# A hybrid decoder layer: all projections ahead of the attention by seven block products, convolution tiles inside it

## The chip, the cores and the metric

The kernel runs on one core of a Trainium2 chip. The time is that of one execution on the device, in microseconds (us). The core's engines work side by side, each through its own queue of instructions: TensorE (PE; its weight loads are listed as PEld), VectorE (DVE), ScalarE (ACT), GpSimd (POOL) and SyncE (SP), which here only starts transfers (DMA).

## What is computed

One layer of a hybrid decoder: a norm, one combined projection into a gated short convolution and an attention, an output projection, and a gated feed-forward part. There are 2048 positions, a model width of 1024, 8 heads of 64, a convolution width of 512 and a feed-forward width of 2816. The reference, cut to this:

```python
h = rms_norm(x, g_mix)
z = h @ w_in
u, gb, gc, q, k, v = jnp.split(z, splits, axis=-1)     # 512 columns each

y_conv = gb * short_conv(gc * u, conv_w)               # causal, width 3

q = rms_norm(q.reshape(B, S, N_HEADS, HEAD_DIM), g_q) * (HEAD_DIM ** -0.5)
k = rms_norm(k.reshape(B, S, N_HEADS, HEAD_DIM), g_k)
y_attn = dilated_mixture(q, k, v)       # branches (128,1), (512,4), (2048,16)

mix = concat(rms_norm(y_conv, g_conv_out), rms_norm(y_attn, g_attn_out))
x = x + mix @ w_out
h = rms_norm(x, g_ffn)
x = x + (silu(h @ w_gate) * (h @ w_up)) @ w_down
```

## The kernel before

All matmuls take float16 operands and add in float32. A float32 operand is split into a high and a low float16 half, and each product is made of three matmuls: high by high, high by low, low by high (`mm3_steps`, lines 185 to 193; the three lines 190, 191 and 192 are those of every such product).

**Ahead of the attention** (`in_and_conv`, line 403). The 2048 rows of x are normed in sixteen tiles (`norm`, line 275), split and transposed into `self.x`, four chunks of 512 positions. The 512 convolution channels are four tiles of 128. `conv_steps` (line 292) makes one tile: for each chunk three products (gate C, u, gate B) of 24 matmuls of 512 columns, then the convolution and the gating on VectorE and ScalarE. Tiles 0, 1 and 2 are made here. Beside them, the weights of everything that comes later are scaled, split and written to DRAM (`spill`, line 152; `spill_pair`, line 159): the q, k and v columns of the four pairs of heads, the convolution's tile 3, and the output projection. Each needs a maximum over the whole piece (`vmax`, line 89; `pow2`, line 76) and, for each eighth of the rows, one ScalarE and one VectorE instruction (lines 148 and 149).

**The attention** (`attention_pairs`, line 727). The heads go in four pairs. `qkv_steps` (line 481) projects one pair: sixteen tiles of 128 rows by 384 columns (q, k and v of both heads), 24 matmuls each; ScalarE copies q and k out of PSUM and squares them (lines 506 and 507), VectorE splits v (line 511), and for every four tiles the norms are made on VectorE and ScalarE (lines 518 to 526), applied and split on GpSimd (lines 527 to 539) and the halves transposed by DMA from SBUF (`transpose`, line 195). `regroup` (line 554) orders q for the dilated branches on GpSimd. `attn_steps` (line 575) then yields twenty steps for each head. In a step TensorE makes scores (line 644), VectorE adds a mask (line 649), ScalarE takes the exponential (line 651) and the high half (line 656), VectorE makes the low half (line 657), and TensorE multiplies by v (line 662). The branch outputs go through DRAM to reorder them and are combined on GpSimd (lines 597 to 605).

**What sets the order.** Pair 0 is projected before the attention starts. In the attention of pair g the projection of pair g + 1 is the filler: after each attention step the generator of the filler is advanced by `RATES[g]` steps (a step is three matmuls), and the filler may not run more than `lag` attention steps ahead (`issue_after`). In the last pair the filler is `tail_steps` (line 778): convolution tile 3, and the first two parts of the output product. A list scheduler orders each engine's queue from this program order.

Behind the attention come the rest of the output product (`out_b`, line 845) and the feed-forward part (`ffn`). The feed-forward part already uses seven block products in place of eight: matrices are cut into two by two blocks, sums of blocks are made beforehand (`winograd_s`, line 942), and the seven products add into three PSUM banks with sums taken out in between (`ORDER` and `BANK`, lines 954 and 955). `General` is a second, slower form of the layer that runs when a denominator is too small.

## Time and profile before

| | |
|---|---|
| median of 3 runs | 2116.0 us |
| runs | 2111.12 to 2119.64 us |
| profiled execution | 2116.69 us, its span 2115.0 us |
| PE busy | 2020.7 us (96% of the span), 11832 matmuls |
| DVE busy | 1370.6 us (65%) |
| ACT busy | 1009.5 us (48%) |
| POOL busy | 655.2 us (31%) |

The span runs from the first to the last instruction, and the profiled execution is 1.7 us longer than it. Busy time is a share of the whole span, and the parts of the kernel have different limits, so the prediction reads tables of busy time by stage. A matmul is recorded from its start to the end of its way through the array, so neighbours overlap, and a busy TensorE isn't one at its peak; what a matmul costs in a row of them is the distance of two starts. L649 is line 649 of the kernel. A group of instructions is listed by line, engine, operation, what it writes from what it reads, shapes and count, then the busy time, the mean duration in ns, the idle time before them, and what ended that.

### The profile page before, as it was taken

The page shows a single profiled execution, that of the slowest core. Times are in us where ns is not written, and L with a number is a line of the kernel's source. Part 1 is how long each engine was busy: PE and PEld are TensorE (multiplying, and loading weights), DVE is VectorE, ACT ScalarE, POOL GpSimd, SP SyncE. Part 2 cuts the span into 40 slices and gives each one's busy share as a digit, 9 for nine tenths or more (in the row PEclk, how much of TensorE's full clock was granted, in tenths as well). Part 3 has the DMA queues.
Part 4 walks back from the last instruction along what each step waited for, and adds up shares of the span by engine and source line. Part 5 has one row for each costly group of instructions (what it writes and reads, how often), then busy time and mean ns, then how long its engine had stood idle before and what let it go on. Part 6 is the DMA issues. An engine that isn't in the chain of part 4 may idle for free.

```text
span 2115.0 us, 31542 instructions
## 1 busy us (share of the span) xinstructions
PE 2020.7 (96%) x11832; PEld 1020.1 (48%) x11832; DVE 1370.6 (65%) x2563; ACT 1009.5 (48%) x1939; POOL 655.2 (31%) x562
## 2 busy tenths in 40 slices
PE   4899998989899999989999999999999999999998
PEld 2344566766666544434444444444444444444443
DVE  6687425776756767876767676676768575555453
ACT  6443347877867665643333333333433344343341
POOL 0001244555451112212312212231223245555463
PEclk9999999999999999999999999999999999999999
DMA  9866445656675767994323223322332762431442
GB/s 247 176 209 215 151 116 115 152 122 154 123 148 155 213 193 249 269 281 139 108 100 105 94 85 101 115 90 90 110 103 88 273 239 60 143 117 55 149 140 82
DMA packets 452963, 310.53 MB, mean 147 GB/s; under 512 B 256192, under 2 KB 405696, under 8 KB 450368
## 3 DMA queue, kind: packets, MB, share of 16 engines
q1 hardware_dynamic: 435120, 285.27, 48.1%
q10 hardware_dynamic: 17680, 23.16, 3.0%
q8 instruction: 94, 1.54, 0.3%
q14 instruction: 69, 0.57, 0.1%
HBM read 161.11 MB, written 107.41 MB: 127 GB/s over the span
## 4 chain that ended last, share of the span: by engine, by line
PE 60%; DVE 12%; DMA 12%; ACT 6%; issue 4%; SPq 3%; POOL 2%; DVEq 0%; ACTq 0%; POOLq 0%
PE ps L1051 31%; PE ps L1184 15%; PE mm L192 3%; PE mm L191 3%; PE mm L190 3%; SPq L198 2%; DVE et L657 2%; PE s L644 1%; DMA d_u<-u 1%; DMA r<-d_u 1%; DMA wraw<-in_w_in_dram 1%; DVE vm_a L95 1%; ACT sm L651 1%; DMA wraw<-in_w_out_dram 1%; PE av L662 1%
## 5 line engine op out<-in xcount | busy, mean ns | idle before, releaser
L1051 PEld LDWEIGHTS <-w 128*128 128x128 f16 x3696 | 362.2, 98 | 454.7 <-issue 18.5
L1051 PE MATMUL ps<-b,w 128*128 128x512 f16 x2112 | 466.2, 381 | 12.3 <-DMA b<-d_h 4.5
L1184 PE MATMUL ps<-b,w 128*128 128x512 f16 x1848 | 399.7, 379 | 3.2 <-DVE x L1192 1.6
L1051 PE MATMUL ps<-hb,w 128*128 128x512 f16 x1584 | 347.3, 379 | 1.5 <-DVE s L1057 1.5
L1184 PEld LDWEIGHTS <-w 128*128 128x128 f16 x1848 | 180.8, 98 | 221.9 <-issue 4.3
L944 POOL TENSOR_TENSOR t<-wq 128x512 f32<-128x512 f32 (+1 forms) x46 | 59.7, 1297 | 410.8 <-issue 234.0
L190 PE MATMUL mm<-wq,b 128*128 128x384 f16 x512 | 168.8, 330 | 7.7 <-DVE vs L511 7.7
L657 DVE TENSOR_TENSOR et<-sm,et 128x512 f16<-128x512 f32 (+1 forms) x160 | 140.8, 893 | 52.7 <-ACT et L656 52.0
L1057 DVE TENSOR_TENSOR s<-ps,s 128x512 f32<-128x512 f32 x220 | 150.1, 683 | 35.8 <-PE ps L1051 35.3
L191 PE MATMUL mm<-wq,b 128*128 128x384 f16 x512 | 168.7, 329 | 0.0
L192 PE MATMUL mm<-wq,b 128*128 128x384 f16 x512 | 168.7, 329 | 0.0
L1191 POOL TENSOR_TENSOR x<-x,s 128x512 f32<-128x512 f32 x72 | 103.5, 1437 | 170.8 <-DVE s L1205 132.7
L651 ACT ACTIVATE sm<-s,bound,kap 128x512 f32<-128x512 f32 (+1 forms) x160 | 120.3, 763 | 39.8 <-DVE s L649 36.7
L1192 DVE SCALAR_TENSOR_TENSOR x<-ps,a_u,x 128x512 f32<-128x512 f32 x96 | 71.8, 749 | 99.0 <-PE ps L1184 72.3
L961 ACT CAST w<-t 128x512 f16<-128x512 f32 x88 | 53.7, 616 | 132.0 <-PE ps L1051 78.6
L191 PEld LDWEIGHTS <-b 128*128 128x128 f16 x768 | 75.9, 99 | 64.7 <-issue 11.1
L190 PE MATMUL cvx<-b,wq 128*128 128x512 f16 (+1 forms) x200 | 76.1, 384 | 31.1 <-DMA b<-ka 24.6
L662 PE MATMUL av<-v,et 128*128 128x65 f16 x1800 | 88.2, 195 | 18.5 <-DVE et L657 15.4
L649 DVE TENSOR_TENSOR s<-s,mask 128x512 f32<-128x512 f32 (+1 forms) x128 | 81.8, 652 | 36.8 <-PE s L644 35.8
L192 PEld LDWEIGHTS <-b 128*128 128x128 f16 x768 | 75.8, 99 | 59.9 <-issue 2.3
L190 PEld LDWEIGHTS <-b 128*128 128x128 f16 x768 | 75.9, 99 | 57.6 <-issue 1.7
L662 PEld LDWEIGHTS <-et 128*128 128x128 f16 x1800 | 78.5, 98 | 42.4 <-DVE et L657 20.1
(295 smaller groups left out, 3539.6 us busy)
## 6 DMA issues: line engine op xcount, KB each, us to landing
d_a<-a ACTq DMA_DIRECT2D x88, 256.0 KB, 2.0
d_wd<-w SPq DMA_DIRECT2D x77, 256.0 KB, 2.1
wq<-d_a SPq DMA_DIRECT2D x64, 256.0 KB, 4.0
b<-d_wd SPq DMA_DIRECT2D x14, 1024.0 KB, 6.5
wraw<-in_w_in_dram SPq DMA_DIRECT2D x24, 512.0 KB, 7.0
d_h<-hl SPq DMA_DIRECT2D x24, 512.0 KB, 3.2
wq<-in_w_gate_dram SPq DMA_DIRECT2D x22, 512.0 KB, 5.1
wq<-in_w_up_dram SPq DMA_DIRECT2D x22, 512.0 KB, 5.3
```

The source lines that it names most:

```text
L190: self.pe = mm(ps, lhsT=lh(k), rhs=rh(k), start=k == ks[0], stop=False)
L191: mm(ps, lhsT=lh(k), rhs=rl(k), start=False, stop=False)
L192: mm(ps, lhsT=ll(k), rhs=rh(k), start=False, stop=k == ks[-1])
L649: nc.vector.tensor_tensor(sp[:, 0:o], sp[:, 0:o], self.masks[b][:, 512 - o:512], op=ALU.add)
L651: nc.scalar.activation(e, sp[:, 0:o], AF.Exp, scale=self.kap, bias=self.bound)
L657: nc.vector.tensor_tensor(et[:, 1], e, et[:, 0], op=ALU.subtract)
L662: self.pe_av = nc.tensor.matmul(av[:, us.index(u)], lhsT=p_, rhs=v_, start=n_ == 0, stop=n_ == len(ops) - 1)
L1051: nc.tensor.matmul(ps[self.BANK[n]], lhsT=w[:, x, k], rhs=b[:, y, k], start=first and k == 0 and q == 0, stop=k == 3 and q == 2, skip_grou ...
L1057: nc.vector.tensor_tensor(t, x, y, op=ALU.add)
L1184: nc.tensor.matmul(ps[self.BANK[n]], lhsT=L[n][:, x, f], rhs=B[n][:, f, y], start=first and f == 0 and q == 0, stop=f == n_f - 1 and q == ...
L1191: nc.gpsimd.tensor_tensor(o, o, s_, op=ALU.add)
L1192: nc.vector.scalar_tensor_tensor(o, bank, u, o, op0=ALU.mult, op1=ALU.add)
```

## The change

The fast path moves into a class of its own, `Fast(Builder)`; `General` keeps the old `qkv_steps`. In `Fast`:

- Ahead of the attention only convolution tile 0 is made. Then all four pairs are projected (`project`), each chunk of 512 rows in two blocks of 256 rows. The rows, the model width and the columns are each cut in two, and seven block products replace eight. A block has 7 x 4 x 3 matmuls of 128 by 192 columns, in three PSUM banks; two pools of banks alternate.
- `sums` makes the sums of blocks of x once for each chunk and splits them. `operands` loads the weights of a pair, scales them, makes the sums of blocks and splits all seven.
- q and k, normed and split, are written to DRAM (`d_qk`), and `load_pair` transposes them from there, one pair ahead, at the start of the branch (1, 1).
- The weights of tiles 1 to 3 and of the output product are prepared between the projections (`SPILLS`), each in smaller pieces than before: nine and four.
- In the attention, `fill` yields the convolution tiles 1 to 3 and then the first parts of the output product; 24 of its steps come before the first attention step, and then 2.2 for each attention step.

```diff
+class Fast(Builder):
+    XS = 8
+    RATE = 2.2
...
+            for step in self.conv_steps(0, W, before):
+                n += bool(step)
+                if not step:
+                    continue
+                if n == 6:
+                    norms.close()
...
+                    with tc.issue_after(self.dve.ins), tc.issue_after(self.sp.ins):
+                        Wn = self.operands(0)
+                elif n in (7, 9):
+                    self.sums(n // 2 - 3, s0)
...
+            for g in range(4):
+                Wg = Wn
+                for i in range(4):
+                    if g == 0 and i < 2:
+                        self.sums(i + 2, s0)
+                    if g < 3 and i == 1:
+                        Wn = self.operands(g + 1)
+                    self.project(g, 3 - i if g == 3 else i, Wg)
+                    if (g, i) == (0, 2):
+                        self.g_out = self.gains(cp, [A["g_conv_out"][0], A["g_attn_out"][0]], "gout", 9)
+                    for k in self.SPILLS.get((g, i), ()):
+                        self.spill_conv(k // 3, k % 3) if k < 9 else self.spill_out((k - 9) // 2, (k - 9) % 2)
...
+    SPILLS = {(0, 3): (0,), (1, 0): (1, 2), (1, 2): (3,), (1, 3): (4,), (2, 0): (5, 6), (2, 2): (7,), (2, 3): (8,),
+              (3, 0): (9, 10), (3, 1): (11, 12)}
+
+    def sums(self, c, s0):
...
+                nc.gpsimd.tensor_tensor(y[i], xh[:, :, o], xl[:, :, o], op=ALU.add)
...
+            v.tensor_tensor(a22, a21, a22, op=ALU.add)
+            v.tensor_tensor(a21, a11, a21, op=ALU.subtract)
+            v.tensor_tensor(a11, a22, a11, op=ALU.subtract)
+            v.tensor_tensor(a12, a12, a11, op=ALU.subtract)
+            for i in range(2):
+                src = y[i].rearrange("p (a k) t -> p a k t", a=2)
+                hi, lo = (Sc[i][:, :, q, :, t * P:(t + 1) * P] for q in range(2))
+                nc.scalar.copy(hi, src)
+                v.tensor_tensor(lo, src, hi, op=ALU.subtract)
+
+    def operands(self, g):
...
+        s, u = self.pow2(self.wsm, self.vmax(raw.rearrange("p k c -> p (k c)")), "w", 11, 11)
...
+        for k in range(KC):
+            nc.scalar.activation(raw[:, k], raw[:, k], AF.Copy, scale=sg[:, k:k + 1])
...
+        def split(n, src):
+            W[n] = self.ring.tile([P, 2, 4, 192], F16, name="w")
+            hi, lo = (W[n][:, q].rearrange("p k (a d) -> p k a d", a=3) for q in range(2))
+            nc.scalar.copy(hi, src)
+            nc.vector.tensor_tensor(lo, src, hi, op=ALU.subtract)
+        p = nc.gpsimd
+        split(0, b11)
+        p.tensor_tensor(b11, b12, b11, op=ALU.subtract)
+        split(2, b22)
+        p.tensor_tensor(b12, b22, b12, op=ALU.subtract)
+        p.tensor_tensor(b22, b22, b11, op=ALU.subtract)
+        split(5, b22)
+        split(4, b11)
+        split(1, b21)
+        p.tensor_tensor(b21, b21, b22, op=ALU.subtract)
+        split(6, b12)
+        split(3, b21)
+        return W
...
+    def project(self, g, c, W):
...
+        n = self.row.rearrange("p (j b d) -> p j b d", j=4, b=4)
...
+        for t in range(2):
+            pool, name = ((self.psmm, "mm"), (self.cvx, "cvx"))[self.units % 2]
+            self.units += 1
+            ps = [pool.tile([P, 512], F32, name=name)[:, 0:192] for _ in range(3)]
...
+            def plus(o, bank, z):
+                nc.vector.scalar_tensor_tensor(o, bank, u, z, op0=ALU.mult, op1=ALU.add)
+            f11, f12, f21, f22 = (f[:, i, h] for i in range(2) for h in range(2))
+            product(0)
+            nc.scalar.activation(f21, ps[0], AF.Copy, scale=u)
+            product(5)
+            plus(f12, ps[1], f21)
+            product(4)
...
+            product(1)
+            nc.scalar.activation(f11, ps[0], AF.Copy, scale=u)
+            product(6)
+            plus(f22, ps[1], f21)
+            plus(f22, ps[2], f22)
+            product(3)
+            plus(f21, ps[1], f21)
+            product(2)
+            plus(f12, ps[2], f12)
...
+            nc.scalar.activation(n[:, j].rearrange("p i (h b) d -> p (i h) (b d)", b=2), fi[:, :, 0:128], AF.Square)
...
+            nc.vector.scalar_tensor_tensor(vl, fv, sv, vh, op0=ALU.mult, op1=ALU.subtract)
...
+    def load_pair(self, g, st):
...
+        for i, (nm, x) in enumerate((("qT", "qT"), ("ka", "ka"), ("kb", "kl"))):
+            st[x] = self.qk.tile([P, 2, S], F16, name=nm, bufs=2)
+            for c in range(4):
+                o = slice(512 * c, 512 * (c + 1))
+                self.transpose(st[x][:, :, o], self.d_qk[g][o, 256 * i:256 * (i + 1)])
...
+    def attention_pairs(self):
...
+        self.load_pair(0, sts[0])
+        self.regroup(sts[0], 0)
+        fill = self.fill()
+        for _ in islice(fill, 24):
+            pass
+        marks, done, lag = [], 0, 12
+        n = 0
+        for g in range(4):
+            for _ in self.attn_steps(g, sts[g], sts[g + 1]):
+                marks.append(self.pe_av.ins)
+                with self.tc.issue_after(marks[n - lag]) if n >= lag else nullcontext():
+                    while done < self.RATE * (n + 1):
+                        next(fill, None)
+                        done += 1
+                n += 1
```

What `project` does for a chunk after its two blocks (the norms of q and k, their scaling, the split) has the instructions of lines 518 to 539. `spill_conv` and `spill_out` are `weights` and `spill_pair` for one ninth and one fourth of their columns or rows.

More of the change, by code (lines that the diff above doesn't have):

```diff
@@ L56 @@
     SHIFTS = (0, 8, 9)
+    XS = 9
     def rnorm(self, pool, ss, n, d, tag, shift=0):
@@ L209, in run @@
             self.d_u = [[dr.tile([S, self.W], F32, name=f"d_u{h}_{b}") for b in range(2)] for h in range(H)]
-            self.d_wq = [dr.tile([P, 2, KC, 384], F16, name=f"d_wq{g}") for g in range(5)]
             self.d_wo = [dr.tile([P, 2, KC, 512], F16, name=f"d_wo{g}") for g in range(2)]
@@ L239, in run @@
         self.otherwise()
-    def check(self):
-        nc = self.nc
-        nc.vector.tensor_single_scalar(self.dmin, self.dmin, 2.0 ** -6, op=ALU.is_lt)
-        nc.vector.tensor_copy(self.low, self.vmax(self.dmin))
-    def otherwise(self):
-        rv = self.nc.values_load(self.low[0:1].bitcast(I32), min_val=0, max_val=0x3F800000,
-                                 skip_runtime_bounds_check_because="it is 0.0 or 1.0")
-        with self.tc.If(rv > 0):
-            General(self.tc, self.A).run()
     def setup(self):
@@ L267, in setup @@
         self.uq = cp.tile([P, 5], F32, name="uq")
-        self.uo = cp.tile([P, 2], F32, name="uo")
+        self.uo = self.uoa = cp.tile([P, 2], F32, name="uo")
         self.ga = cp.tile([P, 2, 4], F32, name="ga")
@@ L391, in conv_end @@
         for m in range(2):
-            nc.vector.tensor_scalar(self.rau[:, m, o], r, u, self.uo[:, m:m + 1], op0=ALU.mult, op1=ALU.mult)
+            nc.vector.tensor_scalar(self.rau[:, m, o], r, u, self.uoa[:, m:m + 1], op0=ALU.mult, op1=ALU.mult)
     def mixer(self, ctx):
@@ L399, in mixer @@
         self.row = rows.tile([P, D], F32, name="row")
-        self.in_and_conv()
-        self.attention()
+        with tc.tile_pool(name="keep", bufs=1) as self.keep:
+            self.in_and_conv()
+            self.attention()
     def in_and_conv(self):
@@ L405, in in_and_conv @@
         w_in, w_out = A["w_in"][0], A["w_out"][0]
+        self.d_wq = [self.dr.tile([P, 2, KC, 384], F16, name=f"d_wq{g}") for g in range(5)]
         with ExitStack() as c:
@@ L685, in pools @@
-    def pools(self, e):
-        tc = self.tc
-        self.pss = e(tc.tile_pool(name="pss", bufs=3, space=PSUM))
-        self.psav = e(tc.tile_pool(name="psav", bufs=2, space=PSUM))
-    def few(self):
-        return self.pss.tile([P, 512], F32, name="s")[:, 0:4]
-    def constants(self, m, u):
-        nc = self.nc
-        self.masks = []
-        for b in range(2):
-            mask = self.at.tile([P, 512], F32, name=f"mask{b}")
-            nc.gpsimd.memset(mask, 0.0)
-            for x in range(4):
-                sg = 1 if x % 2 else -1
-                t = mask[:, x * P:(x + 1) * P].rearrange("p (x a) -> p x a", x=4)
-                pattern = [[32 * sg, 4], [sg, 32]] if b == 0 else [[sg, 4], [4 * sg, 32]]
-                nc.gpsimd.affine_select(t, t, pattern=pattern, compare_op=ALU.is_ge, fill=-1e30, base=0,
-                                        channel_multiplier=-sg)
-            self.masks.append(mask)
-        self.kap = self.at.tile([P, 1], F32, name="kap")
-        nc.vector.tensor_scalar_mul(self.kap, u, HD ** -0.5 * 2.0 ** -22)
-        self.bound = self.at.tile([P, 1], F32, name="bound")
-        nc.vector.tensor_scalar(self.bound, m, -HD ** 0.5, 15 * math.log(2.0), op0=ALU.mult, op1=ALU.add)
@@ L786, in tail_steps, with tail_out @@
         yield from self.conv_steps(3, [self.piece((wt, self.uq[:, 4:5]), m) for m in range(3)], scratch=scratch)
+        yield from self.tail_out()
+    def tail_out(self):
+        nc = self.nc
         self.wo = [self.big.tile([P, 2, 2, D], F16, name=f"b{k}") for k in range(4)]
@@ L1530 @@
     with _tile.TileContext(nc, schedule_with_timeline_sim=True) as tc:
-        Builder(tc, args).run()
+        Fast(tc, args).run()
     r = _run(nc, [arrays], core_ids=[0])
```

604 lines of the change are left out of this document (420 added, 184 removed).

## Prediction

> **What bounds the kernel now.** I first read the table of busy time by stage. Its stretches are cut where the code changes its work: convolution tile 0 ends near 104 us, the first attention scores start at 296, the last attention product ends at 722. The last two rows are short stretches that I use below.
>
> ```profile
> span 2115.0 us, 31542 instructions
> core 0: us, PE busy (x) PEld busy (x) DVE busy (x) ACT busy (x) POOL busy (x), PEclk, DMA share, GB/s
> 0.00:104.00 104.00, 68.50 (x316) 32.52 (x317) 63.32 (x167) 54.89 (x99) 0.91 (x8) 0.98 0.94 215
> 104.00:296.00 192.00, 189.17 (x967) 95.32 (x965) 120.57 (x274) 77.04 (x165) 36.96 (x51) 0.98 0.58 171
> 296.00:722.00 426.00, 398.53 (x4261) 276.08 (x4260) 280.67 (x506) 309.85 (x671) 186.71 (x162) 0.97 0.63 146
> 75.00:100.00 25.00, 23.59 (x109) 10.35 (x107) 14.70 (x17) 4.40 (x8) 0.10 (x1) 1.00 0.87 190
> 875.00:900.00 25.00, 21.73 (x102) 9.78 (x100) 22.78 (x45) 18.05 (x31) 3.62 (x3) 1.00 1.10 303
> ```
>
> After 104 us TensorE is the bound: busy 189 of 192 us while tiles 1 and 2 and the projections of pair 0 run, 399 of 426 us in the attention. VectorE is busy 121 of 192 us, then 281 of 426. The change touches nothing behind 722, so I forecast when the last attention product ends; the remaining 1393 us move with it.
>
> A busy TensorE overlaps its own instructions, so I price matmuls by the distance of their starts, from the timeline:
>
> ```profile
> 39.26 0.38 PE L191 MATMUL cvx<-b,wq 128*128 128x512 f16 x1
> ...
> 44.01 0.38 PE L192 MATMUL cvx<-b,wq 128*128 128x512 f16 x1
> ...
> 400.33 0.22 PE L644 MATMUL s<-qT,ka 128*128 128x128 f16 x1
> ...
> 400.56 0.27 PE L644 MATMUL s<-qT,ka 128*128 128x256 f16 x1
> ...
> 400.89 0.33 PE L190 MATMUL mm<-wq,b 128*128 128x384 f16 x1
> ...
> 404.46 0.33 PE L191 MATMUL mm<-wq,b 128*128 128x384 f16 x1
> ...
> 405.07 1.05 PE L662 MATMUL av<-v,et 128*128 128x65 f16 x29
> 405.96 0.22 PE L644 MATMUL s<-qT,ka 128*128 128x128 f16 x1
> ```
>
> The 512-column ones are 22 starts in 4.75 us, 0.216 us each; the 384-column ones 22 in 3.57, 0.162; four of 128 columns take 0.23, 0.058 each; two of 256 and two of 128 take 0.33, so 0.108 for 256; the 65-column ones take 0.89/29 = 0.031. Each of the narrow ones loads its own weights and is still paced by its columns.
>
> **TensorE's side of the change.** All projections now: 4 pairs x 16 row tiles x 24 = 1536 matmuls of 384 columns, 249 us. After: 4 pairs x 4 chunks x 2 x 7 products x 12 = 2688 matmuls of 192 columns. The width isn't in the trace; a quarter of the way from 128 to 384 columns is 0.058 + 0.026 = 0.084, which gives 226 us. At the 128-column price it would be 156, at the 384-column price 435; the widths in between lie on a line, so I take 226. The gain is 23 us, less than an eighth, since the fixed part of a matmul is paid more often.
>
> The Trainium skill (TensorE: Matmul & The Clock Gate, Back-to-back issue gap) gives about 81 ns for each 128-column matmul in a stream that reloads weights, and 131 for 512. By its line 192 columns would be an estimated 89 ns, 239 us in all; the trace has 58 where the page has 81, so I stay with the trace. By the page, TensorE's own bound in rival 1 would end 13 us later.
>
> The attention after the change holds three convolution tiles (864 matmuls of 512 columns, 186.6 us), the first part of the output product (96, 20.7), scores (688 of 128 columns, 39.9; 256 of 256, 27.6) and weighted values (1800 of 65, 55.8): 331 us. Before it held 1152 of 384 columns (186.6), one tile (288, 62.2), and the same rest: 393 us, and took 426. I keep that ratio: 331 x 426/393 = 359 us. The other ends are 331 (no wait) and 375, should its vector and scalar work crowd together. The vector work there changes little: twelve projection units go, eight convolution chunks come.
>
> **VectorE's side.** What moves in front of the attention, and what is new there, is mostly vector work. Its prices come from the groups of instructions with shapes kept apart (busy us, mean ns of one, idle before):
>
> ```profile
> L657 DVE TENSOR_TENSOR et<-sm,et 128x512 f16<-128x512 f32 x120 | 108.5, 911 | 41.5 <-ACT et L656 41.0
> L657 DVE TENSOR_TENSOR et<-sm,et 128x384 f16<-128x384 f32 x40 | 33.2, 836 | 11.2 <-ACT et L656 11.0
> L962 DVE TENSOR_TENSOR w<-t,w 128x512 f16<-128x512 f32 x88 | 61.0, 698 | 41.7 <-ACT w L961 41.6
> L919 DVE TENSOR_TENSOR hl<-b,hl 128x1024 f16<-128x1024 f32 x16 | 20.3, 1277 | 2.2 <-ACT hl L918 2.2
> L511 DVE SCALAR_TENSOR_TENSOR vs<-mm,vs 128x128 f16<-128x128 f32 x64 | 18.4, 289 | 52.7 <-ACT vs L510 48.4 <-DMA qT<-qkhl 4.2
> L338 DVE SCALAR_TENSOR_TENSOR ka<-cvx,w_un,qT 128x512 f32<-128x512 f32 x12 | 9.0, 747 | 7.2 <-issue 6.3 <-DMA b<-ka 0.5 <-PE cvx L192 0.4
> L518 DVE TENSOR_REDUCE qk_ss<-qkn 128x16 f32<-128x1024 f32 x16 | 19.5, 1218 | 16.6 <-ACT qkn L507 16.4
> L95 DVE TENSOR_REDUCE vm_a<-wraw 128x1 f32<-128x3072 f32 x7 | 23.5, 3350 | 12.5 <-DMA wraw<-in_w_in_dram 10.5 <-issue 2.0
> L177 DVE SCALAR_TENSOR_TENSOR wl<-wraw,w_sg,wh 128x256 f16<-128x256 f32 x16 | 6.8, 483 | 0.0
> L149 DVE SCALAR_TENSOR_TENSOR wq<-wraw,w_sg,wq 128x128 f16<-128x128 f32 x24 | 6.7, 341 | 0.0
> 376.71 0.17 DVE L524 SCALAR_TENSOR_TENSOR qkr_t<-qkr_y 128x16 f32<-128x16 f32 x1
> ```
>
> - A unit (pair, chunk): ten sums out of PSUM, 192 wide, 0.289 + (747-289)/6 ns = 0.365 each; two low halves of v at 0.483; one reduction 1.22; four small ones at 0.17. That is 6.5 us, 16 times: 104.
> - The seven weight operands of a pair: reduction 3.35, 14 small ones 2.4, seven splits of 768 elements at 0.99 (between 698 and 1277 ns): 12.6, four times: 51.
> - The block sums of x, per chunk: eight of 512 at 0.70, four of 1024 at 1.28: 10.7, four times: 43.
> - The convolution weights in nine pieces: reduction 1.22, twelve small ones 2.0, eight products at 0.341: 6.0, nine times: 54.
> - The output weights: two reductions, small ones, and 2 x 1.28 or 8 x 0.483: 8.0, four times: 32.
>
> Sum 284 us. Some of it fits ahead of 104 us: VectorE is idle 10 us of the stretch 75 to 100, and the weights of tile 1 leave that stage (3.35 and some products, 5). There remain 268 us behind 104, against 226 of TensorE. Before, the same 192-us stage had 121 us of vector work; now VectorE is the longer of the two.
>
> Beside it stands GpSimd. Two rows of the timeline:
>
> ```profile
> 377.43 1.90 POOL L527 TENSOR_TENSOR qkn<-qkf,qkr_y 128x1024 f32<-128x1024 f32 x1 [4.05 <-DVE qkr_y L526]
> 378.22 1.66 DVE L657 TENSOR_TENSOR et<-sm,et 128x512 f16<-128x512 f32 x1 [0.93 <-ACT et L656]
> ```
>
> GpSimd runs until 379.33. The vector instruction, which reads two SBUF tensors, starts inside it and ends at 379.88, 0.55 us after GpSimd does; the like instruction at L962 has a mean of 0.698. It looks as if it waited. In the attention L657 costs 120 x (0.911-0.698) + 40 x (0.836-0.55) = 37 us over that (0.55 for 384 elements: three quarters of 698 and a little), with GpSimd busy 187 us: 0.20 us of vector time lost for each us of GpSimd.
>
> ```profile
> L527 POOL TENSOR_TENSOR qkn<-qkf,qkr_y 128x1024 f32<-128x1024 f32 x16 | 31.6, 1974 | 83.7 <-DVE qkr_y L526 76.0 <-DMA d_v<-vs 7.7
> L530 POOL TENSOR_TENSOR qkn<-qkn,gk 128x512 f32<-128x512 f32 x16 | 23.4, 1460 | 0.8
> L538 POOL TENSOR_TENSOR qkhl<-qkn,qkhl 128x256 f16<-128x256 f32 x32 | 24.8, 795 | 0.6 <-ACT qkhl L536 0.6
> L539 POOL TENSOR_TENSOR qkhl<-qkn,qkhl 128x256 f16<-128x256 f32 x32 | 21.4, 688 | 3.8 <-ACT qkhl L537 3.8
> L944 POOL TENSOR_TENSOR t<-wq 128x512 f32<-128x512 f32 x38 | 49.6, 1307 | 410.8 <-issue 234.0 <-DVE w L962 118.0 <-DVE w L965 31.1
> ```
>
> GpSimd's new list: 16 units at 1.97 + 1.46 + 2 x 0.80 + 2 x 0.69 = 6.4 (102 us), 16 weight sums of 768 elements at 1.5 x 1.31 = 2.0 (31), 16 sums of x at 1.97 (32): 165 us. At 0.20 that costs VectorE 33 us; 0 if no such instruction meets GpSimd, 165 if all do. I take 33, the measured rate.
>
> The Trainium skill (GPSIMD Engine Reference, 1. Specifications) states that GpSimd shares its SBUF interfaces with VectorE and contends with vector instructions that have two SBUF inputs. The rows agree. By that rule such vector work (an estimated 15 + 28 + 43 + 25 + 13 = 124 us of the list) and the 165 us would exclude each other, a floor of 289 us; the sum below would be at least 752, and rival 2 would fall.
>
> So the projections take 268 + 33 = 301 us behind 104. TensorE then waits some 75 us. If VectorE keeps only the best share that the table shows, 22.78 of 25, it is 330; without the meetings, 268.
>
> **Costed at nothing.** The transposes of q and k now start from DRAM, 12 for a pair in place of 20, ahead of the v loads on SP's queue:
>
> ```profile
> L198 SPq DMA_TRANSPOSE qT<-qkhl x16: 1237/1273/2382, 262.0 to 622.9; - x16
> ```
>
> At 1.27 us of queue each, 15 us for a pair; a branch of the attention ahead of their use covers that. Without that cover the v load behind them is late, and the weighted values wait: 3 x 15 = 45 us. The new q and k writes, the narrower weight loads and the 24 steps ahead of the attention only fill queues or idle TensorE time. Within a block, product 3 adds to the bank that product 6 has just filled, so it waits for a vector sum of 0.365 us, and everything behind it on TensorE with it; the next block's products use the other pool's banks and can stand in. Without that cover it is 32 blocks x 0.365 = 12 us. The end of tile 0 has no new wait beyond vector work that is counted.
>
> **Sum.** 104 + 301 + 359 = 764 us in place of 722, 42 later. The profiled execution took 2116.69 us, 0.7 over the median of 2116.0: 2159 us.
>
> **Rivals.**
> 1. *TensorE stays the bound* while the projections run; the vector list overlaps better than I price it. Then 104 + 226 + 359 = 689, 33 earlier: 2084 us. For it: only the ten sums of each unit (58 us in all) must come at once to free PSUM; the rest could drift. Against it: 268 exceeds 226 by nearly a fifth before any meeting with GpSimd, and the spills' buffers are closed before the attention opens. It decides once the vector list falls under 226. 0.17.
> 2. *The meetings cost nothing*, and VectorE never idles: 104 + 268 + 359 = 731, 9 later: 2126. For it: the scheduler may place GpSimd's work beside reductions and PSUM reads. Against it: the two rows above. 0.12.
> 3. *One buffer serializes the units.* The squares, the reduction, the four small steps and GpSimd's seven all use the one row tile, 1.22 + 0.7 + 6.4 = 8.3 us without ScalarE's steps, and its next user on ScalarE stands ahead of copies that free PSUM. It decides once queueing stretches that past the unit's 18.8 us (301/16). If the twelve units that have a spill or operands beside them each lose 6.0 us, one piece of weights: 72 more, 2231. For it: the chain crosses three engines ten times. Against it: it has 10 us to spare. 0.15.
>
> That the change does less than it says is settled above: seven eighths of the products give 23 us of 249, no more.
>
> **Chances.** The forecast has 0.56. About 0.5% (10.6 us) is what a measurement of this kernel can tell from no change. Faster: rival 1 and a little of the others' lower tails, 0.18. Same: rival 2, 0.12. Slower: forecast and rival 3, 0.70. The range reaches down to rival 1's middle, leaving out its faster half, and up almost to rival 3: with 330 us for the projections and 375 for the attention the forecast's own upper end is 2116.7 + 87 = 2204, and rival 3 ends beyond. 2085 to 2225.
>
> **What would show it.** Right: the projections end near 405 us; between 104 and there VectorE is busy over 90% and TensorE about three quarters; the 192-column starts are 0.084 us apart; vector instructions with two SBUF inputs have means above 698 ns per 512; the attention takes near 360 us with a higher TensorE share than VectorE's. Wrong: a projection stage under 260 us, idle VectorE in it, or TensorE's waits there ended by ScalarE held up on the row tile. An attention under 331 us can't be, by TensorE's list.

## The result and the profile after

The changed kernel takes 2208.2 us (median of 4 runs, 2204.0 to 2208.5) beside 2117.3 us for the kernel before on the same chip: a ratio of 1.0429, 95% interval 1.0403 to 1.0455. It is slower by 91 us; the forecast was 42. The profiled span is 2206.7 us, 91.7 longer.

The table of busy time by stage, cut at 104 us as for the kernel before, then where tile 0 now ends (its last gating starts at 124.5; before, at 104.3), where the first reduction of a unit (a pair and a chunk) starts (176), where the weight pieces run out (350), at the last projection (453) and the last attention product (824):

```profile
core 0: us, PE busy (x) PEld busy (x) DVE busy (x) ACT busy (x) POOL busy (x), PEclk, DMA share, GB/s
0.00:104.00 104.00, 58.20 (x261) 27.71 (x262) 90.72 (x184) 62.68 (x104) 31.22 (x29) 0.89 0.74 184
104.00:125.00 21.00, 17.77 (x76) 7.96 (x74) 18.11 (x26) 3.50 (x4) 9.10 (x4) 0.89 0.36 108
125.00:176.00 51.00, 31.47 (x296) 29.36 (x297) 48.53 (x106) 28.21 (x56) 19.58 (x15) 0.77 0.35 109
176.00:350.00 174.00, 135.16 (x1378) 128.79 (x1378) 146.78 (x406) 92.53 (x221) 66.66 (x71) 0.86 0.51 152
350.00:453.00 103.00, 98.26 (x1080) 91.14 (x1078) 50.13 (x121) 43.47 (x99) 44.61 (x50) 0.98 0.76 161
453.00:824.00 371.00, 339.12 (x3683) 221.03 (x3680) 269.92 (x468) 252.09 (x483) 129.53 (x107) 0.96 0.59 146
```

Against the forecast's three terms: 104 us for tile 0 stands as a mark only; from there to the end of the projections it is 349 us in place of 301 (+48), the attention takes 371 in place of 359 (+12), and what is behind takes 1383 in place of 1393 (-10). Together that is the 50 us by which the forecast was short. The time lies inside the stated range, above the 2204 us that the prediction had as its own form's upper end: the range holds it only because it had been drawn up towards rival 3, which is not what happened.

Between 104 and 453 VectorE is busy 18.1 + 48.5 + 146.8 + 50.1 = 264 us, 76% of the time and not over 90%. Up to 350 us it is the fuller of the two: 213 of 246 us, 87%, beside 184 us of TensorE. Behind 350 TensorE is, with 98 of 103 us, and VectorE is half idle. The first projection matmul starts at 132.7 us; TensorE then is busy 263 and idle 63 of the 326 us from 125 to 451. What it waits for there (the sum in us, the times, the longest):

```profile
PE cvx L1237 <- ACT f L1247: 19.7, 9, 4.7
PE mm L1237 <- DVE f L1244: 15.1, 8, 4.1
PE mm L1237 <- ACT w L1171: 11.9, 3, 6.7
PE cvx L1237 <- DVE f L1244: 9.6, 6, 2.8
```

L1237 is the block product, L1247 ScalarE's copy of product 0 out of PSUM, L1244 the vector sum out of PSUM, L1171 the high half of a weight operand. For copies TensorE waits 21 us (19.7, and 1.6 for the other pool), for sums 25 (15.1 + 9.6), nearly all of it ahead of 350. VectorE's waits, from 104 to 453, lie at the other end: 47 of the 57 us for these sums are behind 350.

```profile
DVE f L1244 <- PE cvx L1237: 28.7, 21, 5.7
DVE f L1244 <- ACT f L1247: 20.6, 14, 3.3
DVE vm_a L96 <- DMA t<-in_w_out_dram: 11.3, 6, 3.4
DVE f L1244 <- PE mm L1237: 7.6, 11, 1.2
```

So first TensorE waits, for VectorE's sums, ScalarE's copies and the weight operands, then VectorE waits for TensorE. ScalarE's copy is held up by GpSimd, whose multiplication (L1285) still reads what the copy or the square ahead of it will overwrite, and that multiplication in turn waits for VectorE's last norm step (L1280):

```profile
ACT f L1247 <- POOL row L1285: 30.3, 12, 4.6
POOL row L1285 <- DVE qkr_y L1280: 96.3, 13, 13.6
```

In the timeline, L1285 runs during 14 of these 30.3 us; during 13 GpSimd stands idle. So the ring is VectorE's norms, GpSimd's read, ScalarE's copy, TensorE, and back to VectorE's sums, and the read itself is less than half of what the copy waits.

TensorE's price is as forecast. Its timeline in a full stretch, then where it had waited (start, duration, count):

```profile
427.51 1.15 PE L1237 MATMUL cvx<-w,qT 128*128 128x192 f16 x12
...
434.61 0.82 PE L1237 MATMUL cvx<-w,b 128*128 128x192 f16 x8
```

```profile
242.24 2.08 PE L1237 MATMUL mm<-w,qT 128*128 128x192 f16 x12 [4.08 <-DVE f L1244]
246.04 2.08 PE L1237 MATMUL cvx<-w,b 128*128 128x192 f16 x12 [1.72 <-ACT f L1247]
```

The first fence spans 86 starts in 7.10 us: 0.083 us for a matmul of 192 columns. Behind a wait the same twelve take 2.08 us in place of 1.15, with 0.160 us between starts; the granted clock (the share of its full clock that TensorE was given) of that stretch is 0.86, and 0.77 in the one before. Of the 2687 distances between starts in the projections 289 are near 0.160 us, some 22 us more than at 0.083; in e13 below, where TensorE waits less, 51 are. The Trainium skill (TensorE: Matmul & The Clock Gate, Part 1: The HAM clock gate) has the array at half rate by default and at full rate only after about 3.4 us of steady work; the trace agrees on the two rates. So a wait here costs TensorE more than itself.

The vector groups up to 454 us, to be set beside the prediction's prices (busy us, mean ns of one, idle before):

```profile
L1244 DVE SCALAR_TENSOR_TENSOR f<-cvx,uq,f 128x192 f32<-128x192 f32 x80 | 33.0, 412 | 42.5 <-PE cvx L1237 28.7 <-ACT f L1247 13.2
L1172 DVE TENSOR_TENSOR w<-wq,w 128x768 f16<-128x768 f32 x28 | 30.4, 1089 | 0.7 <-ACT w L1171 0.6
L150 DVE SCALAR_TENSOR_TENSOR t<-t,w_sg,t 128x128 f16<-128x128 f32 x72 | 25.7, 408 | 1.2 <-ACT t L149 1.0
L1268 DVE SCALAR_TENSOR_TENSOR vs<-f,sv,vs 128x256 f16<-128x256 f32 x32 | 18.5, 577 | 4.1 <-ACT vs L1267 4.1
```

A sum is 0.412 (priced 0.365), a split 1.09 (0.99), an eighth of a weight piece 0.408 (0.341), a low half of v 0.577 (0.483). Each is above its price, and yet all of it together is 264 us and not 301, since neighbours in VectorE's queue overlap at their ends: from 125 to 453 us all durations add up to 280 us, and VectorE is busy 245. From 104 to 453 they add up to 300 us, so the 301 was nearly met as a sum of durations, in part by luck: the prices were low, but ahead of 104 VectorE is busy 27 us more than before (90.7 beside 63.3), where the prediction had counted on 10 us of its idle time and 5 us that leave.

### The profile page after: what moved, and what is told of

Same layout as the page of the kernel before. It is cut to its first block, busy times and chain, and to the rows that moved or that the text cites. A ratio compares the mean times of both kernels' runs of the same rounds, so it can differ in the third digit from the quotient of the medians.

```text
span 2206.7 us, 34303 instructions
## 1 busy us (share of the span) xinstructions
PE 2030.8 (92%) x12984; PEld 1115.8 (51%) x12984; DVE 1526.2 (69%) x2893; ACT 1047.4 (47%) x1967; POOL 726.7 (33%) x614
## 4 chain that ended last, share of the span: by engine, by line
PE 46%; issue 5%; DVE 4%; DMA 2%; SPq 2%; ACT 2%; POOL 1%; DVEq 0%; POOLq 0%; ACTq 0%
PE ps L812 28%; PE ps L945 15%; SPq L199 2%; DVE hl L680 1%; PE mm L191 1%; PE mm L192 1%; DVE w L933 1%; PE mm L193 1%; PE ps L191 1%; PE ps L192 0%; PE ps L193 0%; POOL x L952 0%; DMA b<-b 0%; ACT wq L742 0%; DMA wq<-d_a 0%
## 5 line engine op out<-in xcount | busy, mean ns | idle before, releaser
L1511 DVE TENSOR_TENSOR et<-sm,et 128x512 f16<-128x512 f32 (+1 forms) x160 | 126.3, 807 | 41.8 <-ACT et L1510 40.8
L191 PE MATMUL mm<-b,wq 128*128 128x512 f16 x320 | 125.7, 393 | 10.1 <-ACT cg L1360 8.6
L193 PE MATMUL mm<-b,wq 128*128 128x512 f16 x320 | 125.1, 391 | 3.4 <-DVE wq L150 3.4
L1237 PEld LDWEIGHTS <-b 128*128 128x128 f16 x1152 | 107.0, 105 | 40.1 <-issue 37.6
L192 PE MATMUL mm<-b,wq 128*128 128x512 f16 x320 | 125.1, 391 | 0.0
L1516 PE MATMUL av<-v,et 128*128 128x65 f16 x1800 | 80.8, 195 | 18.2 <-DVE et L1511 16.2
L933 DVE TENSOR_TENSOR w<-t,w 128x512 f16<-128x512 f32 (+1 forms) x96 | 74.5, 794 | 32.9 <-ACT w L932 32.5
L846 ACT ACTIVATE sg<-s,w_un 128x512 f32<-128x512 f32 x66 | 47.3, 719 | 104.5 <-DVE s L818 104.5
L923 ACT ACTIVATE wq<-wq,asf 128x512 f32<-128x512 f32 x88 | 56.6, 711 | 81.5 <-DMA wq<-d_a 78.5
L932 ACT CAST w<-t 128x512 f16<-128x512 f32 (+1 forms) x96 | 53.4, 580 | 85.6 <-PE ps L945 59.8
```

The lines of the kernel that those rows point to most:

```text
L191: self.pe = mm(ps, lhsT=lh(k), rhs=rh(k), start=k == ks[0], stop=False)
L192: mm(ps, lhsT=lh(k), rhs=rl(k), start=False, stop=False)
L193: mm(ps, lhsT=ll(k), rhs=rh(k), start=False, stop=k == ks[-1])
L933: nc.vector.tensor_tensor(L[n][:, 1, 0:n_f], src[n], L[n][:, 0, 0:n_f], op=ALU.subtract)
L1237: nc.tensor.matmul(ps[self.BANK[m]], lhsT=left(m, x, k), rhs=W[m][:, y, k], start=m in (0, 5, 4) and k == 0 and q == 0, stop=k == 3 and q ...
L1511: nc.vector.tensor_tensor(et[:, 1], e, et[:, 0], op=ALU.subtract)
```

## The experiments

Theory 1: the vector work of the block form, most of it ahead of and in the first half of the projections, sets their time. Theory 2: VectorE and GpSimd take time from each other. Theory 3: the one row tile chains ScalarE to GpSimd. Theory 4: TensorE, or the order alone. All edits are on the changed kernel unless another is named. The table gives what the runs measured; "from" and "to" are the starts of the first and the last matmul of the projections, "attention" that of its last product, in us of the profiled execution. The outputs of e5, e6, e8 and e13 are not the layer's; there the test that would start the slower second form is left out too.

| kernel | from | to | attention | median us | ratio to before (95%) |
|---|---|---|---|---|---|
| before | - | - | 722.2 | 2117.3 | 1 |
| changed | 132.7 | 451.1 | 823.7 | 2208.2 | 1.0429 (1.0403 to 1.0455) |
| e1, eight products | 103.8 | 383.9 | 749.0 | 2143.5 | 1.0145 (1.0104 to 1.0187) |
| e2, pieces later | 131.4 | 453.6 | 822.1 | 2210.0 | 1.0442 (1.0402 to 1.0482) |
| e3, more TensorE | 131.4 | 452.8 | 826.9 | 2215.0 | 1.0484 (1.0444 to 1.0523) |
| e4, more VectorE | 133.0 | 458.9 | 829.1 | 2213.6 | 1.0459 (1.0422 to 1.0495) |
| e5, pieces once | 131.5 | 408.8 | 779.3 | 2171.4 | 1.0272 (1.0238 to 1.0306) |
| e6, no GpSimd | 130.9 | 397.8 | 764.7 | 2159.3 | 1.0231 (1.0198 to 1.0264) |
| e7, squares in PSUM | 130.8 | 434.4 | 799.7 | 2192.9 | 1.0381 (1.0352 to 1.0410) |
| e8, sums once | 110.6 | 431.0 | 804.2 | 2193.0 | 1.0380 (1.0349 to 1.0411) |
| e9, e7 with more GpSimd | 132.2 | 446.6 | 816.3 | 2211.7 | 1.0471 (1.0442 to 1.0500) |
| e10, e1 with pieces spread | 104.2 | 388.1 | 753.7 | 2145.7 | 1.0155 (1.0127 to 1.0183) |
| e11, e10 with squares in PSUM | 103.1 | 377.9 | 746.6 | 2138.8 | 1.0121 (1.0092 to 1.0149) |
| e12, e11 with pace 2.0 | 106.8 | 377.3 | 736.1 | 2128.3 | 1.0078 (1.0050 to 1.0106) |
| e13, four cuts at once | 111.8 | 374.9 | 740.5 | 2127.8 | 1.0058 (1.0040 to 1.0076) |
| e14, e11 with pace 1.8 | 106.7 | 380.0 | 726.3 | 2125.8 | 1.0056 (1.0036 to 1.0075) |
| e15, e7 with pace 2.0 | 130.6 | 435.0 | 793.8 | 2181.3 | 1.0315 (1.0289 to 1.0342) |

Medians from different groups of runs stand beside different runs of the kernel before (2111 to 2117 us), so small differences are better read from the ratios. In the changed kernel, e2 to e7, e9 and e15, whose work up to there is alike, the projections start between 130.6 and 133.0: marks of single profiles repeat to about a microsecond each way.

### e1: the order kept, the seven products undone

```diff
+            nc.vector.scalar_tensor_tensor(W[:, 1, k], raw[:, k], sg[:, k:k + 1], W[:, 0, k], op0=ALU.mult, op1=ALU.subtract)
...
-            product(0)
...
-            plus(f12, ps[2], f12)
+                self.mm3(ps, lambda k: xh[:, k, sl], lambda k: xl[:, k, sl], lambda k: W[:, 0, k], lambda k: W[:, 1, k])
```

`sums` and the block sums of the weights go too, and the ring holds two tiles of a whole pair.

> Keeps the new order (all projections ahead of the attention, convolution tiles 1 to 3 inside it) and undoes the block form alone: every projection is again eight block products as plain 384-column matmuls, without block sums of x and of the weights. Theory 1 (vector work of the block form is bunched in front of the projections and of their first half): convolution tile 0 ends near 105 us again in place of 124.5, the projections are then TensorE's, 1536 matmuls of 0.162 us or 249 us and some gaps, so they end near 380 us in place of 452.5, and the whole is near 2135 us (2125 to 2150), that is 60 to 85 us below the changed kernel. Theory 4 (the order costs: convolution tiles inside the attention, long attention): at most 20 us come back, above 2185 us.

The projections end 67 us sooner and the ratio falls by 0.0284, 60 us of 2115. So two thirds of the loss belong to the block form and one third to the new order with all that e1 keeps of it. The projections start at 103.8, as expected. Their stages in e1:

```profile
104.00:300.00 196.00, 175.78 (x1027) 103.68 (x1026) 148.45 (x438) 103.32 (x292) 56.94 (x77) 0.94 0.80 209
300.00:384.00 84.00, 84.00 (x519) 50.56 (x518) 17.60 (x54) 37.38 (x105) 34.92 (x42) 1.00 0.30 94
```

TensorE is busy 260 of 280 us. That is theory 1's picture, and it excludes theory 4's "at most 20 us".

### e2: the weight pieces later

```diff
-    SPILLS = {(0, 3): (0,), (1, 0): (1, 2), (1, 2): (3,), (1, 3): (4,), (2, 0): (5, 6), (2, 2): (7,), (2, 3): (8,),
-              (3, 0): (9, 10), (3, 1): (11, 12)}
+    SPILLS = {(1, 3): (0,), (2, 0): (1,), (2, 1): (2,), (2, 2): (3,), (2, 3): (4, 5), (3, 0): (6, 9),
+              (3, 1): (7, 8), (3, 2): (10, 11), (3, 3): (12,)}
```

> The later weight pieces are only brought in later (one per unit from unit 7 on in place of two from unit 3 on), the work is the same. Theory 1 (vector work bunched in front while VectorE is half idle behind 348 us): the projections end 15 to 25 us sooner, near 430 to 437 us in place of 452.5, and the whole is 15 to 25 us below the changed kernel. Theory 2 (what costs is the time that VectorE and GpSimd take from each other, wherever it lies) and theory 3 (the one row tile chains the units): within 5 us of the changed kernel.

Nothing is gained, so theory 1 in the form "bunched in front" falls; theories 2 and 3 had said as much (within 5 us). The last stretches of e2:

```profile
125.00:176.00 51.00, 33.50 (x343) 31.51 (x344) 41.96 (x95) 26.98 (x49) 19.21 (x14) 0.82 0.21 64
176.00:350.00 174.00, 134.16 (x1454) 129.70 (x1454) 146.24 (x378) 89.86 (x221) 73.42 (x79) 0.89 0.46 140
350.00:455.00 105.00, 93.37 (x953) 85.00 (x952) 64.93 (x154) 46.29 (x105) 40.42 (x43) 0.92 0.84 188
```

By 350 us TensorE is 1454 - 1378 + 343 - 296 = 123 matmuls ahead of the changed kernel (the two stretches' counts in both tables), some 10 us. Behind 350 the pieces hold up units that were TensorE's own: it stands 12 us there in place of 5, its clock is 0.92 in place of 0.98, and a matmul has 98 ns of busy time (93.37/953) in place of 91 (98.26/1080). All that was won is given back. By an estimate from the means above and the prediction's counts, a unit has 7 us of vector work of its own, 3 us as its share of a pair's operands and 6 to 8 for a piece: more than TensorE's 14 us for a unit, wherever the piece lies.

### e3 and e4: more work for one engine

```diff
             product(0)
+            product(0)
```

```diff
             plus(f12, ps[1], f21)
+            plus(f12, ps[1], f21)
```

> The first product of each group is computed twice (the second time over the first): 384 more matmuls of 192 columns, 32 us of TensorE at 0.083 us each, the result is unchanged. Theory 1: some 105 us of the 320 us of projections (behind 348 us) are bound by TensorE, so a third of the 32 us shows, 8 to 16 us. Theory 4 (TensorE bounds the projections throughout): 30 to 35 us. Theory 3 (the row tile's chain): under 8 us.

> One vector sum of each unit is done twice into the same place: 32 more sums of 0.41 us, 13 us of VectorE spread evenly over the projections, the result is unchanged. Theory 1: the share ahead of 348 us (9 of 16 units) shows, 5 to 10 us. Theory 4 (TensorE throughout): under 3 us. Theory 2 adds nothing to it, since the sum reads PSUM and was not lengthened by GpSimd's work.

32 us more for TensorE move the projections' end by 1.7 us; 13 us more for VectorE move it by 7.8, inside theory 1's 5 to 10. The whole went up by 12 and 6 us by the ratios, 7 and 5 by the medians; the intervals of the ratios overlap with the changed kernel's. Most of e3's matmuls ran where TensorE would have waited, and made it wait less: it is busy 279 us in place of 263, and its clock is 0.93 in place of 0.88.

```profile
125.00:453.00 328.00, 279.09 (x3104) 269.08 (x3105) 249.05 (x625) 163.39 (x372) 132.97 (x136) 0.93 0.54 147
```

Theory 4 (30 to 35 us) is out. e3 stayed below theory 1's 8 to 16 us in the stage itself, and inside theory 3's "under 8"; the whole is too unsure to choose between them.

### e5: ten weight pieces left out

The pieces kept are one of the convolution and two of the output product; each is stored in all places of its kind, so the loads stay.

```diff
-        nc.sync.dma_start(self.d_wc[j][:, m], w)
+        for q in range(9):
+            nc.sync.dma_start(self.d_wc[q // 3][:, q % 3], w)
```

> Of the thirteen weight pieces that are prepared beside the projections only three are prepared and stored in all the places of their kind, so ten are left out of VectorE's and ScalarE's work (their values are then those of another piece; the transfers that store and later load them stay): 8 x 6.0 + 2 x 8.0 = 64 us of VectorE less. Theory 1, as it stands after the later pieces gave nothing (VectorE's sum sets the pace of the projections, a piece costs its vector time wherever it lies): the units of 20 us shrink to 14 to 16 us, the projections end near 395 to 412 us in place of 452.5, and the whole is 40 to 60 us below the changed kernel. Theory 3 (the units hang together by the one row tile, which ScalarE waits for): under 15 us.

```profile
125.00:409.00 284.00, 246.72 (x2743) 236.26 (x2744) 187.26 (x420) 139.53 (x298) 130.54 (x136) 0.94 0.56 145
```

The projections end 42 us sooner for 57 us less of VectorE (187 in place of 245). The ratio falls by 0.0157, 33 us, short of the 40 to 60 that theory 1 in its second form had said; the end, 408.8, is inside its 395 to 412, and beyond theory 3's 15 us. TensorE's wait for sums falls from 24.7 to 8.2 us. A piece costs about three quarters of its vector time; the ScalarE work that goes with it (24 us less) was not tried apart.

### e6, e7 and e9: GpSimd

e6 leaves out GpSimd's multiplications and subtractions for q and k. e7 sends the squares to a PSUM bank, so the row tile no longer stands between ScalarE and GpSimd:

```diff
-            nc.scalar.activation(n[:, j].rearrange("p i (h b) d -> p (i h) (b d)", b=2), fi[:, :, 0:128], AF.Square)
+            sq = self.pstr.tile([P, 512], F32, name="tr")
+            nc.scalar.activation(sq.rearrange("p (x d) -> p x d", d=128), fi[:, :, 0:128], AF.Square)
+            nc.vector.tensor_reduce(ss[:, 8 * t:8 * t + 8], sq.rearrange("p (b d) -> p b d", d=HD), axis=AX.X, op=ALU.add)
...
-        nc.vector.tensor_reduce(ss, n.rearrange("p j b d -> p (j b) d"), axis=AX.X, op=ALU.add)
```

e9 is e7 with both subtractions made twice.

> GpSimd's part of the projections is left out (q and k are not multiplied by their norms, their low halves are zero), about 6 us of GpSimd in each of 16 units; everything else stays. Theory 2 (what costs is the time that VectorE and GpSimd take from each other): the lengthening of the vector instructions between 125 and 453 us goes for the most part, 20 to 30 us. Theory 3 (the row tile): GpSimd no longer holds the row tile, 15 to 20 us. Both together 35 to 45 us, and the projections end near 410 us. Theory 1 without meetings (counted vector work alone): under 10 us.

> The squares of q and k go to a PSUM bank in place of the row tile, and their sums are made from there in two reductions in place of one, so ScalarE no longer waits until GpSimd has read the row tile of the unit before; GpSimd's work stays the same. Theory 3: 10 to 20 us below the changed kernel, and TensorE's wait for ScalarE's copies (19.7 us) goes. Theory 1 and theory 2: within 5 us of it.

> Beside the form with the squares in PSUM (2192.9 us): GpSimd makes each low half of q and k twice, 64 more instructions of 0.7 us, 45 us of GpSimd spread over the projections; the result is unchanged. Theory 2 (vector instructions wait for GpSimd's) at the price that follows from the run without GpSimd (34 us for 98 us of GpSimd): 12 to 20 us above that form; at the prediction's price of 0.20 us for each us: 9 us. If only counted vector work matters: within 4 us.

Without GpSimd the projections end 53 us sooner, at 398 where theories 2 and 3 together had said 410, and the ratio falls by 0.0198 (42 us, inside their 35 to 45). Its stage and three of its vector groups:

```profile
125.00:398.00 273.00, 238.29 (x2716) 230.16 (x2717) 224.53 (x623) 157.23 (x372) 41.13 (x31) 0.95 0.67 172
```

```profile
L1243 DVE SCALAR_TENSOR_TENSOR f<-cvx,uq,f 128x192 f32<-128x192 f32 x80 | 32.7, 411 | 11.2 <-PE cvx L1236 10.8
...
L150 DVE SCALAR_TENSOR_TENSOR t<-t,w_sg,t 128x128 f16<-128x128 f32 x72 | 21.2, 345 | 0.3 <-ACT t L149 0.3
L1267 DVE SCALAR_TENSOR_TENSOR vs<-f,sv,vs 128x256 f16<-128x256 f32 x32 | 15.8, 493 | 8.5 <-ACT vs L1266 7.4 <-DMA ka<-d_qk 1.1
```

The two groups that read two SBUF tensors fall from 408 to 345 ns and from 577 to 493; the sums with a PSUM input stay (412, 411). The Trainium skill (SBUF — State Buffer, Who interferes with whom) says just this: a vector instruction with two SBUF inputs contends with a GpSimd instruction that reads SBUF, one with at most one, outside the modes that use both ports, doesn't. The trace agrees. VectorE's busy time falls by 20 us (245 to 225) for 90 us less of GpSimd (131 to 41), 0.22 for each: that is theory 2's part, and the smaller one. On TensorE the 53 us are 28 of idle time (63 to 35) and 25 of busy time (263 to 238), the clock being 0.95 in place of 0.88. Its waits for copies are gone (21.3 to 0.9), those for sums fall from 24.7 to 18.2; and ScalarE's 30.3 us of waiting for GpSimd's multiplication are no more. Leaving GpSimd out also takes it out of the ring, with its own wait for VectorE's norms; how the part that is not VectorE's divides between GpSimd's running and that wait was not tried.

e7 gives 17 us in the projections (ratio down 0.0048, 10 us; the medians 15). Of ScalarE's waits for GpSimd more than half remain:

```profile
ACT f L1248 <- POOL row L1287: 17.7, 8, 3.7
```

The row tile is out of this chain now. What remains is the tile f, of which there are three, and which GpSimd reads late; that was not taken away by itself. TensorE's wait for the copies fell from 21.3 to 14.7 us, it did not go. In e9, 43 us of GpSimd more (135.7 to 178.8) put 12 us on the projections and 19 us on the whole (2211.7 against 2192.9): theory 2 had 12 to 20, the prediction's price 9. The number fits theory 2, the way does not. VectorE is busy 257 us there and 255 in e7; what grew is TensorE's wait for the copies, from 14.7 to 23.6 us (20.7 below, and 2.9 for the other pool). So e9 prices the ring, not VectorE's lost time.

```profile
PE cvx L1238 <- ACT f L1248: 20.7, 8, 7.2
```

### e8: the block sums of x once

```diff
-        Sc = self.sums_of[c]
+        Sc = self.sums_of[0]
```

> The block sums of x are made for the first chunk only and used for all four (so three quarters of the projections are computed from other sums): 3 x 10.7 = 32 us of VectorE and 24 additions of 2.5 us on GpSimd less, ahead of the projections and in their first units. Theory 1: convolution tile 0 ends near 108 to 114 us in place of 124.5 and the projections 20 to 30 us sooner. Theory 4 (the order of the work, not the sums, delays tile 0): tile 0 stays above 120 us and the projections' end moves by under 12 us.

The calls that make the sums of the other chunks go too: twelve additions on GpSimd, not the 24 that were expected. The projections start 22 us sooner and end 20 us sooner (ratio down 0.0049, 10 us). The first 104 us of e8:

```profile
0.00:104.00 104.00, 66.41 (x302) 31.95 (x303) 70.42 (x174) 57.57 (x99) 14.43 (x21) 0.95 0.84 206
```

VectorE is busy 70 us there, 91 in the changed kernel, 63 before. One wait of TensorE in tile 0 of the changed kernel tells how the sums reach it:

```profile
PE cvx L191 <- DMA b<-kb: 11.5, 2, 8.2
```

It waits for rows of x, whose norms share VectorE's queue with the sums; it is 5.2 us in e8. Theory 1 holds; theory 4's 12 us is passed.

### e13: the four cuts at once

Pieces as in e5, sums as in e8, GpSimd as in e6, squares as in e7.

> Four cuts at once in the seven-product form: ten weight pieces left out, the block sums of x made for one chunk only, GpSimd's part of q and k left out, squares in PSUM (so the outputs are not the layer's; transfers and matmuls stay). If these four are all that holds the projections up, TensorE sets their time: 2688 matmuls of 0.083 us or 223 us from some 112 us on, so they end at 340 to 352 us in place of 452.5 and the whole is near 2100 us. If something else paces them (the operands of the pairs, the chain from TensorE to ScalarE to VectorE inside a unit, or the clock of TensorE): above 370 us.

```profile
112.00:375.00 263.00, 236.00 (x2718) 228.84 (x2717) 175.65 (x429) 129.60 (x290) 35.95 (x30) 0.97 0.65 165
```

The projections end at 375, above the 340 to 352 of a stage that is TensorE's alone and above the 370 beyond which something else was to pace them. TensorE is busy 236 of 263 us. Of the 27 us left it waits 14 for sums, 4 for copies and 4 for weight operands. So four cuts leave the hand-over inside a block; that it is this which remains is read from the waits, no run takes it away. Taken one by one they gave 42, 20, 53 and 17 us, 132 in all; together they give 76: e5, e6 and e7 shorten the same waits, and TensorE's own 223 us, from 112 on, would have ended at 335, so that no more than 116 us were to be had. And this bare form, with most of its side work left out, is still at 1.0058 (1.0040 to 1.0076) of the kernel before.

### e10, e11, e12, e14, e15: where the rest lies, and the best version

e10 spreads the pieces of e1 one to a unit, e11 adds e7's squares in PSUM. e12 and e14 are e11, and e15 is e7, with another pace of the filler:

```diff
-    RATE = 2.2
+    RATE = 2.0
```

> The eight plain products in the new order, with the weight pieces spread one to a unit. A unit there has 3.5 us of vector work and 15.6 us of TensorE, so a piece of some 7 us fits beside it. Theory 1: the projections become TensorE's throughout and end 10 to 20 us sooner than with two pieces in some units (2143.5 us), near 368 to 375 us in place of 385. If pieces cost wherever they lie, as they did in the seven-product form: within 5 us of 2143.5 us.

> As the eight spread products, with the squares in a PSUM bank too. Theory 3 (the row tile): a few us less where TensorE has slack, 0 to 8 us below the form without it. Theory 1 alone: the same.

> As the one before, with 2.0 in place of 2.2 filler steps for each attention step, so that some 32 filler steps (20 us of TensorE) are left to run behind the last attention step, where TensorE waited 14 us for the last normed outputs. 5 to 14 us less if that wait is covered by them; 0 or a loss if the attention steps then wait more for ScalarE and VectorE. With all of it the order alone would cost nothing against the kernel before: near 2115 us.

> The eight spread products with squares in PSUM, and 1.8 filler steps for each attention step (2.2: 2138.8 us, 2.0: 2128.3 us). If the wait behind the last attention step is what the filler covers, 11 us of it are left, so 4 to 10 us less than with 2.0; if the attention steps now lack cover, the same or more.

> The seven-product form with the squares in PSUM (2192.9 us) and 2.0 filler steps for each attention step: the attention's part of the miss. If the pace of the filler inside the attention costs what it did in the eight-product form, 8 to 14 us less; if the attention's 371 us come from VectorE and ScalarE, within 4 us.

Spreading gives nothing in e10 either (388 us, 1.0155). e11 ends the projections 10 us sooner than e10. The slower filler moves the attention's end by 6 us in e15, and the ratio by 0.0066 (14 us), as expected; by 0.0043 (9 us) in e12, which stays 0.8% above the kernel before; near 2115 us, no loss, was expected if all of the wait went. With 1.8 the attention ends 10 us sooner still (726.3), but the filler that is left over runs behind it, and the whole stays (2125.8 and 2128.3), the second of the two cases that were expected. e15's two stages, the second up to the first feed-forward product:

```profile
435.00:794.00 359.00, 338.71 (x3714) 220.80 (x3712) 265.55 (x481) 251.14 (x484) 129.52 (x106) 0.99 0.63 157
794.00:959.00 165.00, 150.06 (x675) 66.99 (x675) 122.31 (x239) 99.08 (x181) 32.70 (x33) 0.95 0.77 226
```

In e7, cut at the same events, they are 365 and 172 us. No version beat the kernel before; e14, the new order with eight products, comes nearest at 1.0056 (1.0036 to 1.0075).

## Why the prediction was wrong

- **The step that failed** is "the projections take 301 us behind 104". It laid VectorE's counted work end to end and took that for the stage. VectorE had 264 us of work there, 37 less than priced, and the stage took 349: VectorE idles 33 us up to 350 and 53 behind it. The work isn't spread as the matmuls are. Sums, copies, operands and pieces keep TensorE waiting until 350 us, at 87% of VectorE; what TensorE couldn't do by then (1080 matmuls, 98 us) comes behind. Moving the pieces alone doesn't mend that (e2), for then neither engine is full. One engine's list is a floor; with a hand-over inside each block the time is above it. Two of the prediction's own signs of being wrong stand in the trace: idle VectorE in the stage, and TensorE's waits ended by ScalarE (21 us).
- **"The end of tile 0 has no new wait beyond vector work that is counted"** was wrong by 20 us, and the projections start another 8 us later. Work that I counted as filling VectorE's time behind 104 stood in front of the norms and operands that TensorE needed. Without three chunks' sums the projections start 22 us sooner (e8).
- **Costed at nothing: product 3's wait on the vector sum**, 12 us if its cover were gone. TensorE waits 24.7 us for sums (15.1 + 9.6), product 3's and those that free a bank together. So the cover was partly gone; how much of it is product 3's stays open.
- **The meetings with GpSimd**, 33 us. As a price of VectorE's time they were right: 20 us for 90 us of GpSimd, 0.22 against the 0.20. But taking GpSimd out is worth 53 us of the stage. On TensorE that is 28 us less idle time, 20 of it waits for ScalarE's copies, which had waited for tiles that GpSimd still reads, and 25 us less busy time at a clock of 0.95 in place of 0.88. The forecast's sum has no term for this way, from GpSimd through ScalarE to TensorE; only rival 3 prices it, on the row tile alone. Whether VectorE and GpSimd shut each other out wholly, as the floor of 289 us has it, no run decides.
- **Rival 3** (one buffer serializes the units) was priced at 72 us more. It is real and small: 17 us in e7. I named the row tile; 17.7 us of the same ScalarE wait remain without it, on f as it seems.
- **Rival 1** (TensorE stays the bound) is excluded by e3: 32 us more of TensorE, 1.7 us later. **Rival 2** (no cost of meetings) by e6.
- **TensorE's price** was right: 0.083 us against 0.084 by interpolation, and an estimated 0.089 by the Trainium skill (TensorE: Matmul & The Clock Gate, Back-to-back issue gap). Its saving is 249 - 223 = 26 us, and none of it reached the time: the stretches at half clock alone cost some 22 us of it (TensorE is busy 252 us with the 2688 matmuls, and 230 in e13 with the same).
- **The transposes from DRAM**, costed at nothing, were rightly so: none of TensorE's waits in the attention is put down to them.
- **The attention** took 371 us against 359. Against e7, the pace of the filler is worth 6 us there and 7 us behind it (e15); e7 itself has 365 us, and no run tells why.
- **Behind the attention**, "untouched": the feed-forward part takes 1218 us where it took 1226, with the same TensorE time (1201 and 1202 us busy). Forms with seven and with eight products have it alike; the cause stays open.
- The direction was right for a reason that holds: one eighth of the products is 26 us of TensorE, and the sums, the splits and the GpSimd work that buy it stand on engines that TensorE has to wait for.

## What to carry to other kernels

A list of one engine's work is a floor for a stage; before taking it for the time, ask at which point each engine's share must be done, and what the others can do until then: here VectorE was the fuller engine for the first seven tenths and TensorE for the rest, and the stage took a third more than VectorE's busy time. A change that takes work off TensorE and puts it on engines that TensorE waits for can lose more than the whole of that work. A helper costs through the tiles that it holds, from the moment they are ready for it to the end of its read: look for copies that wait for its reads, and for what the reads wait for.

## What the runs showed that was not expected

- TensorE at half clock behind waits of 2 to 4 us: twelve matmuls in 2.08 us and not 1.15, a granted clock of 0.77 to 0.86 over whole stretches, and 0.93 once more matmuls filled them (e3).
- Vector sums with a PSUM input are not lengthened by GpSimd at all (412 ns with it, 411 without), while low halves read from SBUF are, by 63 and 84 ns in the mean.
- What the cuts win one by one is far from adding up: 132 us one by one, 76 together (e13).
- A number that came true by another way: doubling GpSimd's subtractions cost what theory 2 had said, and VectorE's busy time hardly moved (e9).
